# Segment mean over sorted ids: other places in the stream for looks, bridges and gathers, other places in the queue for the probes, and seven fills on ScalarE

## The chip, the cores and the metric

One core of one Trainium2 chip runs the kernel. The time is device microseconds of one execution. The engines are named as in the profile: DVE (VectorE), ACT (ScalarE), POOL (GpSimd, which also issues the indirect transfers), PE (TensorE, hardly used here) and SP (SyncE, which issues the plain transfers).

## The reference

Ten million values belong to 10,000 segments. The ids are sorted, so a segment is a contiguous stretch of about 1,000 values, and the result is the mean of each stretch:

```
sums = np.zeros(num_segments); counts = np.zeros(num_segments)
np.add.at(sums, segment_ids, data)
np.add.at(counts, segment_ids, 1)
return sums / np.maximum(counts, 1)
```

## The kernel before

Each of the 128 partitions holds 78,125 neighbouring values, cut into 90 **ranges** of 875. Two ranges make a data **tile** (128 x 1750 values, 875 KB); 45 tiles are loaded by SP in the order of `ORDER`: first the even tiles 0, 2, 4, 6, 8, then an odd and an even one in turn. The tile pool has 16 buffers. A range is taken to hold at most one segment boundary. ACT sums each tile (`total`, L557); DVE sums each range up to its boundary (`split`, L566, one instruction per range, 90 in all). Nothing of the ids is loaded whole. Where the boundary lies is found in three ways:

- **Probes** (`load_probes` L211, `load_mids` L216): SP fetches the id of every 175th position, 8 bytes at a time.
- **First look and second look**, for the ranges of even tiles: from the probes DVE works out which 175 ids hold the boundary and writes their places to `IDX` (L403). POOL gathers these ids with one indirect transfer per range (`gather`, L343), ACT adds them up (`add_ids`, L429) and DVE turns the sum into the exact place (`second_look`, L439).
- **Bridge**, for the ranges of odd tiles: with the exact places of the even neighbours on both sides, DVE guesses the boundary by a line between them (`bridge`, L481 to L524; LK at L481 is its first step, IDX at L519 its last but one). POOL gathers 232 ids around the guess, ACT adds them, `bridged` (L532) makes the place exact. Before a bridge POOL works out six small helpers (`prepare`, L455 to L468).

The even tiles are taken in nine **groups**, g0 to g8, of 1, 2, 3, 3, 3, 3, 3, 3 and 2 tiles, with two ranges per tile; a bridge goes with each group from g1 on. The gathered ids lie in a ring of 18 places (`RING`).

Every engine runs its instructions in the order in which the program writes them. The program is written **slot** by slot: slot s holds first the `add_ids` planned for it, then (for even s) the `total` of the next tile, then split s, and then the DVE and POOL steps put behind it (`after[s]`). The table `PLAN` has one row per group: slot and pace of the first look, slot of `prepare`, first slot of the adds of the 175 ids, slot of the second look, slot and pace of the bridge, first slot of the adds of the 232 ids, and slot of `bridged`. A pace of 99 puts all steps into one slot, a pace of 1, 2 or 3 so many steps into each. The first `HEAD` groups are looked at ahead of split 0. The table `POS` does the same for the steps that make counts, sums and outputs. SP's order comes from a list of pieces: each probe transfer has a slot, each data tile too, and a lead (`X_PIECE`, `X_DATA`) says how far ahead they are issued. At most eight of SP's transfers are under way, since the program has eight semaphores for them, and the next waits for the one eight before it; the gathers have eight of their own.

Of the kernel before, what the change touches and what calls it, by code (L numbers as in the profile page):

```python
# [9 lines left out]
FP32 = mybir.dt.float32  # L10
# [12 lines left out]
NR = 90  # L23
# [6 lines left out]
NX = NR + E  # L30
# [9 lines left out]
SEQ = [2 * t + k for t in ORDER for k in (0, 1)]  # L40
AT = {r: s for s, r in enumerate(SEQ)}
GROUPS = [(0, 1), (1, 3), (3, 6), (6, 9), (9, 12), (12, 15), (15, 18), (18, 21), (21, 23)]
X_PIECE = 22
X_DATA = 27
PLAN = [
# [9 lines left out]
]  # L55
POS = {
    "extend": (27, 1),
    "ext_rows": (42, 99),
    "keys": (38, 1),
    "keysx": (40, 2),  # L60
    "taxes": (50, -2),
    "counts0": (52, 2),
    "sums0": (59, 1),
    "head": (69, 2),
    "keys1": (51, 3),
    "counts1": (61, 1),
    "sums1": (62, 1),
    "place": (72, 1),
    "keys2": (59, -2),
    "check": (61, 1),  # L70
    "pick": (77, 2),
    "last": (78, 1),
    "counts2": (76, 2),
    "hits": (81, 1),
    "sums2": (79, 2),
    "spread2": (81, 1),
    "counts3": (81, 3),
    "verdict": (86, -2),
    "verdict1": (87, 1),
    "values": (89, 1),  # L80
    "weights": (82, -2),
    "base": (81, 99),
    "base2": (85, 1),
    "late": (86, 1),
    "place0": (70, 1),
    "recheck": (80, 1),
    "spans": (76, 1),
    "total": (88, 1),
}
# [85 lines left out]
def kernel(  # L175
# [6 lines left out]
    nc = tc.nc  # L182
# [9 lines left out]
    cpool = ctx.enter_context(tc.tile_pool(name="cpool", bufs=1))  # L192
# [35 lines left out]
    q5 = cpool.tile([P, 5, NX + PAD], FP32, name="q5")  # L228
# [5 lines left out]
    def view(ap, dims):  # L234
        return bass.AP(ap.tensor, ap.offset, [list(ap.ap[0])] + dims)

    nc.scalar.activation(  # L237
        out=gt32[:, :, 0 : 2 * WO : 2], in_=view(q5[:, 0, 0:1], [[0, RING], [0, WO]]), func=ACT.Copy
# [30 lines left out]
        out=plast, in0=pc, scalar1=float(P - 1), scalar2=1.0e6, op0=ALU.is_equal, op1=ALU.mult  # L269
# [5 lines left out]
        out=sp_i, in0=sp_i, scalar1=3, scalar2=None, op0=ALU.arith_shift_right  # L275
# [79 lines left out]
    def limits(a, b):  # L355

        def s1():
            need('VI', range(a, min(b + 1, NR)))
            nc.vector.tensor_sub(out=BT[:, a:b], in0=VI[:, a + 1 : b + 1], in1=VI[:, a:b])  # L359

        def s2():
            nc.vector.tensor_scalar(
                out=NB[:, a:b], in0=BT[:, a:b], scalar1=1.0, scalar2=None, op0=ALU.not_equal
            )
            mark('NB', range(a, b))

        return [s1, s2]

    def first_look(i, j):

        last = j == NE
        v = nc.vector
        e = lambda t: own(t, i, j)
        l1, l2 = limits(max(4 * i - 1, 0), min(4 * j - 1, NR))

        def s0():
            if last:
                m = NR * K + 1 - NPR
                v.tensor_copy(
                    out=pr_flat.bitcast(I32)[:, 2 * NPR : 2 * (NPR + m)].rearrange("p (a b) -> p a b", b=2),  # L380
                    in_=view(snt32[:, 0:1], [[0, m], [1, 2]]),
                )
            l1()

        def s1():
            v.tensor_reduce(
                out=e(SG), in_=view(pr32[:, 4 * i, 0:1], [[8 * K, j - i], [2 * K, 2], [2, K]]), axis=AX.X, op=ALU.add
            )

        def s2():  # L390
            v.scalar_tensor_tensor(
                out=e(ST), in0=view(pr32[:, 4 * i + 1, 0:1], [[8 * K, j - i], [2 * K, 2]]), scalar=float(K),
                in1=e(SG), op0=ALU.mult, op1=ALU.subtract,
            )

        def s3():
            need('NB', rows_of(i, j, 0))
            v.scalar_tensor_tensor(
                out=e(ST), in0=e(NB), scalar=FAR, in1=e(ST), op0=ALU.mult, op1=ALU.add
            )  # L400

        def s4():
            v.scalar_tensor_tensor(  # L403
                out=e(IDX), in0=e(ST), scalar=float(S), in1=e(wb), op0=ALU.mult, op1=ALU.add
            )
            if last:
                c = slice(NR - 1, NR)
                v.scalar_tensor_tensor(
                    out=IDX[:, c], in0=ST[:, c], scalar=float(TAIL), in1=wb[:, c], op0=ALU.mult, op1=ALU.add
                )  # L410
            for r in rows_of(i, j, 0):
                gather(r, W)

        def s5():
# [789 lines left out]
    head = len(after[-1])  # L1204
# [21 lines left out]
    t = table(M1, NT1 // 7, tax)  # L1226
# [107 lines left out]
```

## Time and profile before

| | before |
|---|---|
| median of 3 runs | 203.32 us (203.28 to 204.47) |
| the profiled execution, time / span | 204.23 us / 202.5 us |
| DVE busy | 144.7 us (71%), 479 instructions |
| ACT busy | 129.1 us (64%) |
| POOL busy | 120.1 us (59%), 90 gathers of them |
| DMA | 56.69 MB, of these 16.26 MB by the gathers |

The profiled execution took 1.8 us more than its span, and is 0.9 us above the median. The busy shares are averages; which wait ends last has to be read stretch by stretch.

### The profile page before, as it was taken

To read this page: it belongs to the slowest core of one execution; us is meant where nothing else is said; L and a number is where in the kernel's file an instruction comes from. 1 tells how busy PE (TensorE), PEld (TensorE's weight loads), DVE (VectorE), ACT (ScalarE), POOL (GpSimd) and SP (SyncE) were. 2 spreads that over 40 slices of the span, in tenths; PEclk is the share of its full clock that TensorE was granted. 3 is DMA by queue.
4 is the path that set the end of the run, shared out by engine and by line. 5 is a ranking of instruction groups with operands and counts; after the bars stand their busy time and mean duration, and the time that the engine had idled before them with its cause. 6 is when DMAs were issued, how large, how long until landed. Compare 5 with 4: busy or idle time off the path is not lost.

```text
span 202.5 us, 1502 instructions
## 1 busy us (share of the span) xinstructions
PE 1.6 (1%) x6; PEld 1.4 (1%) x6; DVE 144.7 (71%) x479; ACT 129.1 (64%) x283; POOL 120.1 (59%) x183
## 2 busy tenths in 40 slices
PE   0000000000000000100000000000000000000100
PEld 0000000000000000100000000000000000000000
DVE  6540391580599950995957999296999899999972
ACT  8100586551879953966599992666788995891250
POOL 5557777567577065586557177727477606964910
DMA  4979999999999999999999999999999902300000
GB/s 6 182 40 380 344 316 379 341 353 370 373 343 388 366 243 351 389 365 337 382 362 346 373 412 412 409 402 414 405 410 401 394 35 69 97 0 0 0 0 11
DMA packets 47684, 56.69 MB, mean 280 GB/s; under 512 B 37664, under 2 KB 38104, under 8 KB 47671
## 3 DMA queue, kind: packets, MB, share of 16 engines
q1 hardware_dynamic: 41739, 40.32, 60.1%
q0 software_dynamic: 5760, 16.26, 22.5%
q14 instruction: 13, 0.11, 0.1%
q10 hardware_dynamic: 172, 0.00, 0.0%
HBM read 58.97 MB, written 0.04 MB: 291 GB/s over the span
## 4 chain that ended last, share of the span: by engine, by line
DMA 30%; DVE 26%; issue 22%; ACT 9%; POOL 7%; SPq 2%; DVEq 0%; ACTq 0%; POOLq 0%
DMA GT<-in_segment_ids_dram,IDX 17%; DVE junk_v L566 15%; DMA data_t<-in_data_dram 11%; ACT junk_a L557 5%; POOL GT L343 5%; ACT junk_a L429 4%; DMA pr<-in_segment_ids_dram 2%; POOL xa L1056 2%; DVE PS L855 1%; SPq L211 1%; ACT add L1144 1%; POOL pb L1088 1%; DVE ct L863 1%; DVE most L1133 1%; DVE q L439 1%
## 5 line engine op out<-in xcount | busy, mean ns | idle before, releaser
L343 POOL DMA_INDIRECT GT<-in_segment_ids_dram,IDX x90 | 90.9, 1010 | 63.0 <-issue 24.3
L566 DVE SCALAR_TENSOR_TENSOR junk_v<-iota,q,data_t 128x875 bf16<-128x875 f32 x90 | 100.3, 1115 | 0.7
L557 ACT ACTIVATE junk_a<-data_t 128x1750 bf16<-128x1750 f32 (+1 forms) x45 | 74.2, 1650 | 1.4
L429 ACT ACTIVATE junk_a<-GT 128x175 bf16<-128x175 int32 (+1 forms) x90 | 34.5, 383 | 56.4 <-DMA GT<-in_segment_ids_dram,IDX 51.8
L439 DVE SCALAR_TENSOR_TENSOR q<-YY,GS 128x6 f32<-128x6 f32 (+2 forms) x9 | 1.5, 163 | 23.2 <-ACT junk_a L429 22.9
L429 ACT ACTIVATION_READ_ACCUMULATOR junk_a<-GT 128x1 f32 x90 | 16.8, 187 | 0.0
L532 DVE TENSOR_TENSOR q<-ZV,GS 128x6 f32<-128x6 f32 (+1 forms) x8 | 1.3, 162 | 14.8 <-ACT junk_a L429 14.8
L557 ACT ACTIVATION_READ_ACCUMULATOR junk_a<-data_t 128x1 f32 x45 | 8.4, 187 | 0.0
L566 DVE DVE_READ_ACCUMULATOR junk_v<-iota,q,data_t 128x1 f32 x90 | 7.3, 81 | 0.0
L831 ACT ACTIVATE junk_a<-bad 128x272 bf16<-128x272 f32 x1 | 0.4, 430 | 7.6 <-POOL OUT L1062 7.6
L481 DVE TENSOR_TENSOR LK<-q,LN 128x6 f32<-128x6 f32 (+1 forms) x8 | 1.3, 160 | 5.0 <-issue 5.0
L359 DVE TENSOR_TENSOR q<-pr 128x12 f32<-128x12 int32 (+3 forms) x9 | 1.6, 175 | 3.6 <-DMA pr<-in_segment_ids_dram 3.5
L237 ACT ACTIVATE GT<-q 128x4176 int32<-128x4176 f32 x1 | 3.9, 3908 | 0.0
L1056 POOL TENSOR_TENSOR xa<-xa 128x36 f32<-128x36 f32 (+3 forms) x5 | 3.5, 700 | 0.3
L286 DVE CAST jj<-jj_i 128x128 f32<-128x128 int32 x1 | 2.9, 2854 | 0.7 <-POOL jj_i L285 0.7
L855 DVE TENSOR_TENSOR_SCAN PS<-ps,PS 128x20 f32<-128x20 f32 (+2 forms) x4 | 2.8, 708 | 0.1
L1088 POOL TENSOR_TENSOR pb<-pb,RB 128x620 f32<-128x620 f32 x1 | 1.3, 1298 | 2.7 <-DVE RB L873 2.7
L1036 POOL TENSOR_TENSOR xa<-pa,RG 128x720 f32<-128x720 f32 x1 | 1.6, 1636 | 1.5 <-DVE RG L1032 1.5
L462 POOL TENSOR_TENSOR FB<-FB,wb 128x6 f32<-128x6 f32 (+1 forms) x8 | 1.7, 213 | 0.7
L468 POOL TENSOR_TENSOR WV<-wb,WV 128x6 f32<-128x6 f32 (+1 forms) x8 | 1.6, 202 | 0.7
L459 POOL TENSOR_SCALAR FB<-NBP 128x6 f32<-128x6 f32 (+1 forms) x8 | 1.6, 204 | 0.6
L1133 DVE TENSOR_REDUCE most<-add 128x31 f32<-128x930 f32 x1 | 1.1, 1121 | 1.2 <-ACT add L1144 1.2
(158 smaller groups left out, 81.6 us busy)
## 6 DMA issues: line engine op xcount, KB each, us to landing
data_t<-in_data_dram SPq DMA_DIRECT2D x44, 875.0 KB
GT<-in_segment_ids_dram,IDX POOLq DMA_INDIRECT x90
data_t<-in_data_dram SPq DMA_DIRECT2D x1, 562.5 KB
pr<-in_segment_ids_dram SPq DMA_DIRECT2D x22, 11.0 KB
pr<-in_segment_ids_dram SPq DMA_DIRECT2D x3, 6.0 KB
out_dram<-OUT SPq DMA_DIRECT2D x1, 36.6 KB
pr<-in_segment_ids_dram SPq DMA_DIRECT2D x1, 4.0 KB
snt<-in_segment_ids_dram ACTq DMA_DIRECT2D x1, 1.0 KB
```

The costliest lines, as they stand in the source:

```text
L211: nc.sync.dma_start(out=pr_flat[:, a:b], in_=ids_p[:, a * S : (b - 1) * S + 1 : S])
L237: nc.scalar.activation(out=gt32[:, :, 0 : 2 * WO : 2], in_=view(q5[:, 0, 0:1], [[0, RING], [0, WO]]), func=ACT.Copy)
L286: nc.vector.tensor_copy(out=jj, in_=jj_i)
L343: nc.gpsimd.indirect_dma_start(out=GT[:, slots[r], 0:w], out_offset=None, in_=ids2d[:], in_offset=bass.IndirectOffsetOnAxis(ap=IDX[:, r : ...
L429: nc.scalar.activation(out=junk_a[:, 0:w], in_=gt32[:, slots[r], 0 : 2 * w : 2], func=ACT.Copy, accum_out=GS[:, r : r + 1],)
L439: nc.vector.scalar_tensor_tensor(out=e(KK), in0=e(YY), scalar=float(S // K), in1=e(GS), op0=ALU.mult, op1=ALU.subtract)
L557: nc.scalar.activation(out=junk_a[:, 0:n], in_=tiles[t][:, 0:n], func=ACT.Copy, accum_out=T[:, 2 * t : 2 * t + 1])
L566: nc.vector.scalar_tensor_tensor(out=junk_v[:, 0:n], in0=iota[:, 0:n], scalar=KK[:, r : r + 1], in1=d, op0=ALU.is_ge if r % 2 else ALU.is_ ...
L855: nc.vector.tensor_tensor_scan(out=PS[:, a + 1 : b + 1], data0=ps, data1=ps, initial=PS[:, a : a + 1], op0=ALU.max, op1=ALU.max,)
L1056: nc.gpsimd.tensor_tensor(out=m[:, :, 0 : w - h], in0=m[:, :, 0 : w - h], in1=m[:, :, h:w], op=ALU.add)
L1088: e.tensor_tensor(out=pb, in0=pb, in1=view(RB[:, RM : RM + 1], [[0, NC], [1, NW]]), op=ALU.mult)
L1133: nc.vector.tensor_reduce(out=most, in_=add, axis=AX.X, op=ALU.add)
```

## The change

`PLAN` and `POS` get other numbers. `HEAD` is 2, so that the look of g2 moves behind the second look of g0. The look of g0 asks for three probes of its first tile alone (`limits(0, 2)`) and that of g1 for the rest; before, the look of g0 needed a fourth id, which a `load_mids` brings. The probe transfers, of which the first three stood ahead of all data and six more ahead of the second tile, now stand one to three at a time between data tiles. Seven buffers that POOL and its `memset` filled with zeros are filled by ACT, from a zero column of `q5`. `EARLY` is used nowhere.

```diff
-X_PIECE = 22
-X_DATA = 27
+X_PIECE = 24
+Y_PIECE = 0.75
+X_DATA = 26
 PLAN = [
...
-    (2, 1, 3, 3, 4, 4, 2, 10, 17),
-    (1, 99, 14, 5, 9, 20, 2, 25, 29),
+    (-1, 99, 3, 3, 4, 4, 2, 10, 17),
+    (1, 2, 13, 5, 10, 18, 99, 28, 28),
...
-HEAD = 3
-EARLY = 5
+HEAD = 2
+EARLY = 3
...
-        l1, l2 = limits(max(4 * i - 1, 0), min(4 * j - 1, NR))
+        l1, l2 = limits(*((0, 2) if j == 1 else (2 if i == 1 else 4 * i - 1, min(4 * j - 1, NR))))
...
-    nc.gpsimd.memset(tab, 0.0)
-    nc.gpsimd.memset(tax, 0.0)
-    nc.gpsimd.memset(shf[:, :, ND : ND + 1], 0.0)
-    nc.gpsimd.memset(add, 0.0)
-    nc.gpsimd.memset(xa, 0.0)
+    bad = cpool.tile([P, 2 * NX + 8 + 2 * NOD], FP32, name="bad")
+    for t in (tab, tax, shf[:, :, ND : ND + 1], add, xa, nbw, bad):
+        shape = [[0, n] for _, n in list(t.ap)[1:]]
+        nc.scalar.activation(out=t, in_=view(q5[:, 0, 0:1], shape), func=ACT.Copy)
...
-    nc.gpsimd.memset(nbw, 0.0)
...
-    pieces = [(load_probes, (i,), -99 if i < 3 else max(AT[4 * i] - X_PIECE , 1)) for i in range(NE)]
-    pieces += [(load_mids, (0, 4), 0.5)]
-    pieces += [(load_mids, (i, min(i + 6, NOD)), AT[4 * i] - X_PIECE - 1) for i in range(4, NOD, 6)]
+    at = lambda i: max(AT[4 * i] - X_PIECE, 0.5 + (i - 1) * Y_PIECE) if i else -99
+    pieces = [(load_probes, (i,), at(i)) for i in range(NE)]
+    pieces += [(load_mids, (i, min(i + 6, NOD)), at(i + 1) - 0.1) for i in range(4, NOD, 6)]
+    pieces += [(load_mids, (0, 4), 0.4)]
```

**POOL, from its last fills to the gathers of the second bridge.** GT with 175 are gathers of looks, GT with 232 those of bridges; LN, FB, SM and WV are the helpers of `prepare`, with two tiles (2x2) for the bridge of g1 and three (3x2) for that of g2. First before, then now:

```order
L632 MEMSET bad 128x272
L343 DMA GT<-in_segment_ids_dram,IDX 128x175 x12
L455 TENSOR_SCALAR LN<-NBP 128x2x2
L459 TENSOR_SCALAR FB<-NBP 128x2x2
L462 TENSOR_TENSOR FB<-FB,wb 128x2x2
L463 TENSOR_TENSOR SM<-q_74 128x2
L464 TENSOR_SCALAR WV<-pr 128x2x2
L468 TENSOR_TENSOR WV<-wb,WV 128x2x2
L343 DMA GT<-in_segment_ids_dram,IDX 128x175 x6
L455 TENSOR_SCALAR LN<-NBP 128x3x2
```

```order
L629 MEMSET KEY 128x112
L344 DMA GT<-in_segment_ids_dram,IDX 128x175 x6
L456 TENSOR_SCALAR LN<-NBP 128x2x2
...
L344 DMA GT<-in_segment_ids_dram,IDX 128x175 x6
L456 TENSOR_SCALAR LN<-NBP 128x3x2
...
L344 DMA GT<-in_segment_ids_dram,IDX 128x175 x6
L344 DMA GT<-in_segment_ids_dram,IDX 128x232 x10
```

Each `prepare` moved ahead of six gathers; that of g2 stood behind the gathers of g3 and now stands ahead of them.

**ACT, in the slots 21 to 29 of before.** The adds of g4 (175) and of the bridge of g3 (232) between the totals of the tiles (`data_t`). First before, then now:

```order
L429 ACTIVATE junk_a,GS<-GT 128x175 x3
L557 ACTIVATE junk_a,T<-data_t 128x1750
L429 ACTIVATE junk_a,GS<-GT 128x175 x2
L557 ACTIVATE junk_a,T<-data_t 128x1750
L429 ACTIVATE junk_a,GS<-GT 128x232 x2
L429 ACTIVATE junk_a,GS<-GT 128x175
L429 ACTIVATE junk_a,GS<-GT 128x232
```

```order
L430 ACTIVATE junk_a,GS<-GT 128x175 x3
L558 ACTIVATE junk_a,T<-data_t 128x1750
L430 ACTIVATE junk_a,GS<-GT 128x175 x3
L558 ACTIVATE junk_a,T<-data_t 128x1750 x2
L430 ACTIVATE junk_a,GS<-GT 128x232 x6
```

The last add of g4 stood behind two adds of the bridge and now stands ahead of all six.

**SP, the first transfers.** pr with 11 are probes, with 4 and 6 the single ids of `load_mids`, data_t the tiles. First before, then now:

```order
L211 DMA pr<-in_segment_ids_dram 128x11x1 x3
L216 DMA pr<-in_segment_ids_dram 128x6x1
L223 DMA data_t<-in_data_dram 128x1750
L216 DMA pr<-in_segment_ids_dram 128x4x1
L211 DMA pr<-in_segment_ids_dram 128x11x1 x6
L223 DMA data_t<-in_data_dram 128x1750 x2
```

```order
L212 DMA pr<-in_segment_ids_dram 128x11x1
L224 DMA data_t<-in_data_dram 128x1750
L217 DMA pr<-in_segment_ids_dram 128x4x1
L212 DMA pr<-in_segment_ids_dram 128x11x1 x3
L224 DMA data_t<-in_data_dram 128x1750
L212 DMA pr<-in_segment_ids_dram 128x11x1
L217 DMA pr<-in_segment_ids_dram 128x6x1
L212 DMA pr<-in_segment_ids_dram 128x11x1
L224 DMA data_t<-in_data_dram 128x1750
```

One probe instead of three stands ahead of the first tile, and the second tile has four probes ahead of it instead of nine.

The other moves, in words (slots before, then now). The places of a first look are all written in slot 47, then 48 for g7, in 25, then 23 for g5, in 39, then 35 for g6. The bridge of g3 ran over the slots 20 to 23 and stands whole in 18; that of g4 over 29 to 31 and stands whole in 29; that of g5 begins in 42, then 40; that of g6 in 53, then 52; that of g8 in 72, then 69. The second looks stand in 9, 25, 34, 48 (g3 to g6), now in 10, 24, 32, 47, and those of g7 and g8 stay in 56 and 68; `bridged` stands in 29, 40, 53 (g3 to g5), now in 28, 41, 52.

## Rows read from the trace of the kernel before

**Rows 1.** Page, parts 1, 3 and 5: engines, a DMA queue (packets, MB), gathers.

```profile
PE 1.6 (1%) x6; PEld 1.4 (1%) x6; DVE 144.7 (71%) x479; ACT 129.1 (64%) x283; POOL 120.1 (59%) x183
...
q0 software_dynamic: 5760, 16.26, 22.5%
...
L343 POOL DMA_INDIRECT GT<-in_segment_ids_dram,IDX x90 | 90.9, 1010 | 63.0 <-issue 24.3
```

**Rows 2.** Timeline of DVE, waits: start, us, instruction, shapes [idle before <-releaser].

```profile
10.24 0.17 DVE L359 TENSOR_TENSOR q<-pr 128x3 f32<-128x3 int32 x1 [2.50 <-DMA pr<-in_segment_ids_dram]
...
21.15 0.16 DVE L439 SCALAR_TENSOR_TENSOR q<-YY,GS 128x2 f32<-128x2 f32 x1 [7.23 <-ACT junk_a L429]
...
37.69 0.17 DVE L481 TENSOR_TENSOR LK<-q,LN 128x6 f32<-128x6 f32 x1 [4.98 <-issue]
...
52.44 0.16 DVE L532 TENSOR_TENSOR q<-ZV,GS 128x4 f32<-128x4 f32 x1 [7.39 <-ACT junk_a L429]
...
80.73 0.17 DVE L439 SCALAR_TENSOR_TENSOR q<-YY,GS 128x6 f32<-128x6 f32 x1 [7.21 <-ACT junk_a L429]
...
96.34 0.17 DVE L439 SCALAR_TENSOR_TENSOR q<-YY,GS 128x6 f32<-128x6 f32 x1 [2.47 <-ACT junk_a L429]
107.26 0.17 DVE L532 TENSOR_TENSOR q<-ZV,GS 128x6 f32<-128x6 f32 x1 [3.43 <-ACT junk_a L429]
...
131.48 0.17 DVE L532 TENSOR_TENSOR q<-ZV,GS 128x6 f32<-128x6 f32 x1 [3.72 <-ACT junk_a L429]
...
139.58 0.17 DVE L439 SCALAR_TENSOR_TENSOR q<-YY,GS 128x6 f32<-128x6 f32 x1 [1.91 <-ACT junk_a L429]
```

**Rows 3.** Timeline of POOL: some of its gathers, and one helper (LN).

```profile
12.01 1.27 POOL L343 DMA_INDIRECT GT<-in_segment_ids_dram,IDX  x1 [4.36 <-DVE YY L415]
...
26.63 1.00 POOL L343 DMA_INDIRECT GT<-in_segment_ids_dram,IDX  x1 [0.30 <-issue]
27.70 0.20 POOL L455 TENSOR_SCALAR LN<-NBP 128x4 f32<-128x4 f32 x1
...
29.78 1.09 POOL L343 DMA_INDIRECT GT<-in_segment_ids_dram,IDX  x1 [0.59 <-DVE LL L488]
...
41.67 1.08 POOL L343 DMA_INDIRECT GT<-in_segment_ids_dram,IDX  x1 [2.83 <-DVE CC L514]
...
71.63 1.08 POOL L343 DMA_INDIRECT GT<-in_segment_ids_dram,IDX  x1 [5.43 <-ACT junk_a L429]
```

**Rows 4.** Timeline of ACT: the first fill, and adds that waited for a gather.

```profile
2.04 3.91 ACT L237 ACTIVATE GT<-q 128x4176 int32<-128x4176 f32 x1
...
15.89 0.36 ACT L429 ACTIVATE junk_a<-GT 128x175 bf16<-128x175 int32 x1 [9.94 <-DMA GT<-in_segment_ids_dram,IDX]
...
32.07 0.36 ACT L429 ACTIVATE junk_a<-GT 128x175 bf16<-128x175 int32 x1 [0.18 <-DMA GT<-in_segment_ids_dram,IDX]
...
78.84 0.41 ACT L429 ACTIVATE junk_a<-GT 128x232 bf16<-128x232 int32 x1 [5.12 <-DMA GT<-in_segment_ids_dram,IDX]
```

**Rows 5.** Timeline of DVE, start: two casts.

```profile
2.97 0.21 DVE L254 CAST rp<-rp_i 128x110 f32<-128x110 int32 x1
...
4.88 2.85 DVE L286 CAST jj<-jj_i 128x128 f32<-128x128 int32 x1 [0.73 <-POOL jj_i L285]
```

**Rows 6.** Timeline of DVE: splits 29, 41, 54, 57 and the last instruction.

```profile
85.05 1.13 DVE L566 SCALAR_TENSOR_TENSOR junk_v<-iota,q,data_t 128x875 bf16<-128x875 f32 x1
...
108.25 1.12 DVE L566 SCALAR_TENSOR_TENSOR junk_v<-iota,q,data_t 128x875 bf16<-128x875 f32 x1
...
132.61 1.03 DVE L566 SCALAR_TENSOR_TENSOR junk_v<-iota,q,data_t 128x875 bf16<-128x875 f32 x1
...
140.49 1.12 DVE L566 SCALAR_TENSOR_TENSOR junk_v<-iota,q,data_t 128x875 bf16<-128x875 f32 x1
...
198.21 0.27 DVE L1157 SCALAR_TENSOR_TENSOR OUT<-gb,q,most 128x31 f32<-128x31 f32 x1
```

**Rows 7.** One stretch: us, length; busy PE, PEld, DVE, ACT, POOL; PEclk, DMA share, GB/s.

```profile
0.00:120.00 120.00, 0.98 (x4) 0.93 (x4) 75.19 (x259) 76.69 (x169) 74.06 (x120) 1.00 1.01 321
```

More of the change, by code (lines that the diff above doesn't have):

```diff
@@ L42 @@
 GROUPS = [(0, 1), (1, 3), (3, 6), (6, 9), (9, 12), (12, 15), (15, 18), (18, 21), (21, 23)]
-X_PIECE = 22
-X_DATA = 27
+X_PIECE = 24
+Y_PIECE = 0.75
+X_DATA = 26
 PLAN = [
[9 rows of a table removed]
[9 rows of a table added]
 ]
 POS = {
-    "extend": (27, 1),
-    "ext_rows": (42, 99),
-    "keys": (38, 1),
+    "extend": (30, 1),
+    "ext_rows": (45, 99),
+    "keys": (35, 99),
     "keysx": (40, 2),
     "taxes": (50, -2),
-    "counts0": (52, 2),
-    "sums0": (59, 1),
-    "head": (69, 2),
+    "counts0": (50, 2),
+    "sums0": (61, 1),
+    "head": (72, 99),
     "keys1": (51, 3),
[L66 to L70, printed above, removed]
+    "counts1": (54, 1),
+    "sums1": (63, 1),
+    "place": (71, 1),
+    "keys2": (60, 3),
+    "check": (61, -2),
     "pick": (77, 2),
-    "last": (78, 1),
-    "counts2": (76, 2),
-    "hits": (81, 1),
+    "last": (77, 2),
+    "counts2": (76, 1),
+    "hits": (82, -2),
     "sums2": (79, 2),
@@ L79 @@
     "verdict1": (87, 1),
-    "values": (89, 1),
-    "weights": (82, -2),
+    "values": (89, 2),
+    "weights": (82, 1),
     "base": (81, 99),
     "base2": (85, 1),
-    "late": (86, 1),
-    "place0": (70, 1),
+    "late": (87, -2),
+    "place0": (72, 1),
     "recheck": (80, 1),
-    "spans": (76, 1),
-    "total": (88, 1),
-}
-HEAD = 3
-EARLY = 5
+    "spans": (74, 3),
+    "total": (88, 99),
+}
+HEAD = 2
+EARLY = 3
 RING = 18
@@ L621 @@
     nc.vector.memset(RF, 0.0)
-    nc.gpsimd.memset(tab, 0.0)
-    nc.gpsimd.memset(tax, 0.0)
-    nc.gpsimd.memset(shf[:, :, ND : ND + 1], 0.0)
-    nc.gpsimd.memset(add, 0.0)
-    nc.gpsimd.memset(xa, 0.0)
+    bad = cpool.tile([P, 2 * NX + 8 + 2 * NOD], FP32, name="bad")
+    for t in (tab, tax, shf[:, :, ND : ND + 1], add, xa, nbw, bad):
+        shape = [[0, n] for _, n in list(t.ap)[1:]]
+        nc.scalar.activation(out=t, in_=view(q5[:, 0, 0:1], shape), func=ACT.Copy)
     nc.vector.memset(PS[:, 0:1], 0.0)
     nc.vector.memset(PX[:, 0:1], 0.0)
-    nc.gpsimd.memset(nbw, 0.0)
     nc.gpsimd.memset(KEY, -1000.0)
-    bad = cpool.tile([P, 2 * NX + 8 + 2 * NOD], FP32, name="bad")
-    nc.gpsimd.memset(bad, 0.0)
     j1 = cpool.tile([P, NX], FP32, name="j1")
```

14 rows, old and new, of the table PLAN are left out of this document.

## The prediction, made before the changed kernel ran

> **What bounds the kernel now.** I read the busy shares first: no engine is busy for more than 71% of the span, and 90 gathers with 16.26 MB run beside the data [rows 1]. An average of 71% hides two halves, so I went on to the waits of DVE, which ends the kernel [rows 2]. They stand between 10 and 140 us, and nearly all have one releaser: the ACT add of a gathered set of ids. The large ones are 7.23 us at 21.15 (second look of g0), 4.98 at 37.69 (LK, the first step of the bridge of g2), 7.39 at 52.44 (`bridged` of g1), 7.21 at 80.73 (second look of g4), then 2.47, 3.43, 3.72 and 1.91. Split 57 starts at 140.49 and the last DVE instruction at 198.21 [rows 6]; the waits of that tail that I read are short, so I take its 57.7 us as DVE's own work. POOL tells why the adds are late [rows 3]: gathers follow each other at (26.63 - 12.01) / 11 = 1.33 us, so POOL is the metronome of the first 60 us, and its first gather goes out only at 12.01. A gather lands some time later, seen where an ACT add waits for it [rows 4]: 12.01 to 15.89 = 3.9 us for the first, 26.63 to 32.07 = 5.4, 71.63 to 78.84 = 7.2. So the first half is a chain: look on DVE, gather on POOL, landing, add on ACT, second look on DVE. What starts it earlier, or takes a queue out of it, moves all behind it, up to the point where another resource binds.
>
> **The change, part by part.** All times are in the profiled execution's own span.
>
> *Start.* Before, the first wait of DVE ends at 10.24, for probes, and the gather follows 1.77 later [rows 2, 3]. Two things now come earlier. The cast of `jj` took 2.85 us beside POOL's fills, a like cast 0.21 [rows 5]; with the fills gone from POOL it should take about 0.2, and DVE stands at the look from about 4.88 + 0.3 = 5.2. And the look of g0 needs only the one probe transfer ahead of the first data tile. When that lands no row shows: at the earliest DVE is ready at 5.2, at the latest it is 10.24 again. I take 5.5, near the first, since one transfer stands where three stood with a tile before the fourth id: gather 0 at 5.5 + 1.8 = 7.3. ACT's seven fills hold 2839 elements per partition; at 3.91 us for 4176 [rows 4] that is 2.7 us, up to 4 with seven starts. They end near 10, ahead of the first landing at 7.3 + 3.9 = 11.2, which is their cover; without it they would cost at most those 4 us once.
>
> *g0 to g2.* g1's look needs the later probes; I put it at 9 and its four gathers at 10.4 to 15.7. Gather 1 (8.6) lands at 12.5 to 15.8, so the second look of g0 stands at 13.2 to 16.5, and the look of g2, now behind it, 1.8 later. POOL meanwhile does `prepare` of g1, which takes 27.70 to about 29.2, 1.5 us [rows 3]. g2's gathers so start between 17.4 and 18.2; I take 17.8. Before, they were the seventh to twelfth in the row: 12.01 + 6 x 1.33 = 20.0. The gain is only 2.2, since the wait of 7.23 gets a successor of its own.
>
> The first landing of 3.9 us was measured while few gathers were under way, the 7.2 in the saturated stretch [rows 4]. The Trainium skill, page "DMA: Bandwidth & Descriptors", section "Queues, rings and completion order", says that each DMA engine goes round-robin between the queue rows that have work, packet by packet. By it an earlier gather shares every engine with the tiles at once, and this speaks against the whole gain of an earlier start; with 7.2 instead of 3.9 the second look of g0 stands at 16.5 and g2's gathers start at 18.2, 0.4 later than the sum has them. No run here shows yet which it is.
>
> *The bridge of g1.* Before, `prepare` of g2 stood behind g3's six gathers, and LK waited 4.98 for it. Now it stands ahead of them: g2's gathers end at 17.8 + 8.0 = 25.8, `prepare` at 27.1 to 27.3, g3's gathers at 35.1. LK's wait goes, and the bridge of g1 has its places written by then, so its first gather is at 35.1 (41.67 before [rows 3]). Its `bridged` ended its wait 52.44 - 41.67 = 10.77 after that; the same behind 35.1 gives 45.8. Gain 6.6; with the places 1.3 late, 5.3.
>
> *g3, g4, bridge of g3.* Sixteen gathers (four and six of two bridges, six of g4) take 35.1 + 21.3 = 56.4; the second look of g3, now in slot 10, waits about 1.3 for an add that stands ahead of it, and the gathers of g4 slip by some 1.7; `prepare` adds 1.5, the bridge of g3 in one piece about 1.2. Its first gather is at 60.8, before at 71.63 [rows 3]. On ACT the last add of g4 no longer stands behind adds of the bridge: that order was the wait of 7.21 at 80.73 [rows 2]. So DVE runs 45.8 + (85.05 - 52.44 - 7.21) + 1.3 + 0.5 = 73.0 on its own work to split 29 [rows 2, 6], while the last gather of the bridge, at 67.4, needs 7.2 to land and 0.6 for the add, 75.2: a new wait of some 2.2, split 29 at 75.4. **Gain 9.6.**
>
> *g5.* Its gathers run from 67.4 + 1.33 + 1.5 = 70.3 to 77.0; with 7.2 + 0.6 the second look of g5 stands at 84.8, a wait of about 3. Before, from that step at 96.34 six splits took 108.25 - 96.34 - 3.43 = 8.48, 1.41 each; now eight splits follow, 11.3, and some four small steps that moved ahead, at 0.99 / 5 = 0.2 each (the five between 107.26 and 108.25 [rows 2, 6]). Split 41 at 84.8 + 11.3 + 0.8 = 96.9. **Gain 11.35.**
>
> *Splits 41 to 57.* Before 132.61 - 108.25 - 3.72 = 20.64 of work to split 54 [rows 2, 6]; seven steps have moved in (1.4): 118.9. Its wait of 3.72 should vanish, the gathers of that bridge having the two slots by which it begins earlier. To split 57 there are 140.49 - 132.61 - 1.91 = 5.97, four more steps (0.8) and a wait of 1.5 to 2, since the second look of g7 stays in its slot: 127.5. **Gain 13.0.**
>
> *The tail.* 57.7 us less the 1.2 of six steps now ahead of it. Gain 14.2 at most. Against that I set 1.2: at 120 us the stream has moved 120 x 321 = 38.5 MB [rows 7], and splits 54 to 56, now near 120, need 28 tiles, which come just in time. **Gain 13.0**: 204.23 - 13.0 = 191.2 in the profile's own time, which stands 0.9 above the median of the runs; so 190.3, and I say **190.5 us**.
>
> The spread probes, the casts and the moved table steps of the tail add no instruction. The probe transfers pass data tiles in SP's queue; before, no split waited for data, so a tile delayed by 11 KB transfers costs nothing as long as that slack lasts, which is what the 1.2 and the first rival are for.
>
> **Rivals.**
>
> (a) *The data stream becomes the bound.* At about 118 us some 37.9 MB have moved. Of these about 69 gathers take 69 x 16.26 / 90 = 12.5 MB [rows 1], which leaves 25.4 MB, or 28 tiles of 0.9 MB, several of them in flight, not landed. Split 53 needs 27 whole tiles. For it: a faster DVE does not raise the 321 GB/s [rows 7]. Against: no split before waited for a tile. If DVE is held by about 5 us there, the end is near 195.5. Chance 0.16.
>
> (b) *The bunched adds bring waits back.* `bridged` of g3 and g5 and the second look of g5 stand in slots 28, 52 and 32 behind adds of a whole group; if landings take 2 to 3 us longer than 7.2 at three of them, 8 us go: 198.5. For it: every wait in the list has this releaser. Against: gathers themselves start 8 to 11 us earlier there. Chance 0.10.
>
> (c) *The gain is handed back entirely*, by (a) and (b) in turn or because g0's probe lands at 10 us as before: 201.5 to 205. Chance 0.09.
>
> (d) *Slower.* All looks stand in DVE's order ahead of splits that need nothing of them. The probes that a look reads now wait in SP's queue behind data tiles, and some looks come earlier (g5 in slot 21, before 24; `Y_PIECE` and `X_PIECE` place the transfer). A look that meets an absent probe stops DVE, its splits and its gathers too. The only such wait before was 2.50 at 10.24 [rows 2]. It decides once it eats the whole 13 and 2 more: about 3 us at each of five looks, which gives 206 to 210. For it: eight transfers at a time, each tile 0.9 MB or 2.8 us at 321 GB/s, so a probe behind eight places lands 22 us after its turn. Against: `X_PIECE` of 24 slots, at 1.2 us or more, leaves 29. Chance 0.09.
>
> **How the numbers follow.** The forecast has 0.56. The lower end is the forecast less what I allowed for: without the 1.2 for data, the 2.2 at split 29 and 1 at the start, 186. The upper end must take in (a) and (b), 200, and leaves out (c), (d) and a little. Range **186 to 200**. About 1% (2 us) is what a measurement of this kernel can tell from no change. Faster by over 1%, below 201.3: the forecast, (a) and (b), 0.82. Within 1%: most of (c), 0.08. Slower: (d) and the rest, 0.10.
>
> **What the new profile would show.** The cast of `jj` at 0.2 us, the first gather at 7.3, the first wait that an ACT add ends no later than 16.5; no wait at LK of g2; `bridged` of g1 at 45.8; no wait of 7 us at the second look of g4; splits 29, 41, 54 and 57 at 75.4, 96.9, 118.9 and 127.5; the last DVE instruction at 185. Wrong: a wait of DVE or ACT whose releaser is `data_t` shows (a), one at L360 for `pr` shows (d), waits above 4 us at slots 28, 32 or 52 show (b). If the first gather stays near 12 us the start has failed and the rest shrinks by up to 4.5 us.

## The result and the profile after

The changed kernel takes **187.08 us** (median of 4 runs, 185.92 to 188.99) against 203.42 beside it; the ratio is 0.916 with a 95% interval of 0.909 to 0.923. Ratios here and below are taken over the fast runs alone (here without 188.99 and with a fifth run of 186.27), so they are not the quotients of the medians shown. A second comparison gave 187.17 us and 0.920 (0.913 to 0.927). Forecast were 190.5 us and a range of 186 to 200. The profiled execution took 188.09 us with a span of 186.3.

The page of the changed kernel first, parts 1 and 5 (busy us, mean ns | idle time ahead and what ended most of it):

```profile
PE 1.6 (1%) x6; PEld 1.4 (1%) x6; DVE 143.3 (77%) x479; ACT 131.9 (71%) x290; POOL 117.3 (63%) x176
...
L567 DVE SCALAR_TENSOR_TENSOR junk_v<-iota,q,data_t 128x875 bf16<-128x875 f32 x90 | 100.6, 1118 | 5.7 <-DMA data_t<-in_data_dram 5.1
...
L440 DVE SCALAR_TENSOR_TENSOR q<-YY,GS 128x6 f32<-128x6 f32 (+2 forms) x9 | 1.5, 171 | 12.3 <-ACT junk_a L430 12.3
L533 DVE TENSOR_TENSOR q<-ZV,GS 128x6 f32<-128x6 f32 (+1 forms) x8 | 1.9, 232 | 9.0 <-ACT junk_a L430 9.0
L360 DVE TENSOR_TENSOR q<-pr 128x12 f32<-128x12 int32 (+3 forms) x9 | 1.6, 175 | 6.1 <-DMA pr<-in_segment_ids_dram 6.0
```

Two lines of the page before, for the splits and for the first step of the looks:

```profile
L566 DVE SCALAR_TENSOR_TENSOR junk_v<-iota,q,data_t 128x875 bf16<-128x875 f32 x90 | 100.3, 1115 | 0.7
...
L359 DVE TENSOR_TENSOR q<-pr 128x12 f32<-128x12 int32 (+3 forms) x9 | 1.6, 175 | 3.6 <-DMA pr<-in_segment_ids_dram 3.5
```

DVE is busy for nearly as long as before (143.3 us, 144.7 in [rows 1]) and for a larger share, so what was saved is waiting. What waiting is left for adds is 12.3 + 9.0 us, and a new kind has come: 5.1 us for data tiles, where before no split waited for one. The looks wait 6.1 us, mostly for probes, where it was 3.6.

The timeline of DVE in the changed kernel (columns as in [rows 2]): the cast of `jj`, the larger waits, and two steps that no longer wait, LK of g2 at 30.05 and the second look of g4 at 66.37:

```profile
4.87 0.23 DVE L287 CAST jj<-jj_i 128x128 f32<-128x128 int32 x1 [0.72 <-POOL jj_i L286]
...
8.78 0.17 DVE L360 TENSOR_TENSOR q<-pr 128x9 f32<-128x9 int32 x1 [2.59 <-DMA pr<-in_segment_ids_dram]
15.03 0.16 DVE L440 SCALAR_TENSOR_TENSOR q<-YY,GS 128x2 f32<-128x2 f32 x1 [5.32 <-ACT junk_a L430]
16.42 0.18 DVE L360 TENSOR_TENSOR q<-pr 128x12 f32<-128x12 int32 x1 [1.23 <-DMA pr<-in_segment_ids_dram]
...
29.78 0.17 DVE L440 SCALAR_TENSOR_TENSOR q<-YY,GS 128x6 f32<-128x6 f32 x1 [2.26 <-ACT junk_a L430]
30.05 0.17 DVE L482 TENSOR_TENSOR LK<-q,LN 128x6 f32<-128x6 f32 x1
...
45.54 0.20 DVE L533 TENSOR_TENSOR q<-ZV,GS 128x4 f32<-128x4 f32 x1 [6.87 <-ACT junk_a L430]
...
66.37 0.23 DVE L440 SCALAR_TENSOR_TENSOR q<-YY,GS 128x6 f32<-128x6 f32 x1
...
71.39 1.13 DVE L567 SCALAR_TENSOR_TENSOR junk_v<-iota,q,data_t 128x875 bf16<-128x875 f32 x1 [1.33 <-DMA data_t<-in_data_dram]
74.67 0.23 DVE L533 TENSOR_TENSOR q<-ZV,GS 128x6 f32<-128x6 f32 x1 [2.15 <-ACT junk_a L430]
82.74 0.17 DVE L440 SCALAR_TENSOR_TENSOR q<-YY,GS 128x6 f32<-128x6 f32 x1 [1.17 <-ACT junk_a L430]
95.08 1.13 DVE L567 SCALAR_TENSOR_TENSOR junk_v<-iota,q,data_t 128x875 bf16<-128x875 f32 x1 [2.63 <-DMA data_t<-in_data_dram]
...
124.85 0.17 DVE L440 SCALAR_TENSOR_TENSOR q<-YY,GS 128x6 f32<-128x6 f32 x1 [0.46 <-ACT junk_a L430]
```

Against [rows 2]: the wait at LK and that of 7.21 us at the second look of g4 are gone. `bridged` of g1 still waits, 6.87 us, but ends at 45.54 instead of 52.44. The waits of 3.43 and 3.72 at `bridged` of g4 and g5 are gone too.

POOL in the changed kernel: the first gather, the first and last of g2, the first of the bridges of g1 and g3:

```profile
7.07 1.26 POOL L344 DMA_INDIRECT GT<-in_segment_ids_dram,IDX  x1 [2.10 <-DVE YY L416]
...
17.57 1.09 POOL L344 DMA_INDIRECT GT<-in_segment_ids_dram,IDX  x1 [1.18 <-DVE IDX L404]
...
24.17 0.99 POOL L344 DMA_INDIRECT GT<-in_segment_ids_dram,IDX  x1 [0.30 <-issue]
...
35.14 0.99 POOL L344 DMA_INDIRECT GT<-in_segment_ids_dram,IDX  x1 [0.30 <-DMA GT<-in_segment_ids_dram,IDX]
...
59.80 1.08 POOL L344 DMA_INDIRECT GT<-in_segment_ids_dram,IDX  x1 [1.84 <-ACT junk_a L558]
```

They answer to [rows 3]: 12.01 became 7.07, 41.67 became 35.14, 71.63 became 59.80. ACT in the changed kernel, the last fill and the add of the first gather (as [rows 4]):

```profile
8.52 0.41 ACT L626 ACTIVATE bad<-q 128x272 f32<-128x272 f32 x1
13.44 0.36 ACT L430 ACTIVATE junk_a<-GT 128x175 bf16<-128x175 int32 x1 [4.51 <-DMA GT<-in_segment_ids_dram,IDX]
```

The fills end at 8.9, with 4.51 us to spare. The first gather took 13.44 - 7.07 = 6.4 us to land, 3.9 before. The Trainium skill, page "DMA: Bandwidth & Descriptors", section "Queues, rings and completion order", has each DMA engine go round-robin between the queues that have work; the trace agrees in so far as a gather among tiles and probes took nearer 7.2 than 3.9; between issue and add the DMA engines moved 204 GB/s now and 96 before.

The splits 29, 41, 54 and 57 and the last instruction of DVE in the changed kernel (as [rows 6]):

```profile
74.83 1.12 DVE L567 SCALAR_TENSOR_TENSOR junk_v<-iota,q,data_t 128x875 bf16<-128x875 f32 x1
...
97.30 1.13 DVE L567 SCALAR_TENSOR_TENSOR junk_v<-iota,q,data_t 128x875 bf16<-128x875 f32 x1
...
119.20 1.13 DVE L567 SCALAR_TENSOR_TENSOR junk_v<-iota,q,data_t 128x875 bf16<-128x875 f32 x1 [0.20 <-DMA data_t<-in_data_dram]
...
126.44 1.13 DVE L567 SCALAR_TENSOR_TENSOR junk_v<-iota,q,data_t 128x875 bf16<-128x875 f32 x1
...
182.01 0.27 DVE L1154 SCALAR_TENSOR_TENSOR OUT<-gb,q,most 128x31 f32<-128x31 f32 x1
```

The lead is 10.2 us at split 29, 11.0 at 41, 13.4 at 54, 14.1 at 57 and 16.2 at the end.

### The profile page after: what moved, and what is told of

It is laid out like the page before. It is cut to its first block, busy times and chain, and to the rows that moved or that the text cites. A ratio compares the mean times of both kernels' runs of the same rounds, so it can differ in the third digit from the quotient of the medians.

```text
span 186.3 us, 1505 instructions
## 1 busy us (share of the span) xinstructions
PE 1.6 (1%) x6; PEld 1.4 (1%) x6; DVE 143.3 (77%) x479; ACT 131.9 (71%) x290; POOL 117.3 (63%) x176
## 4 chain that ended last, share of the span: by engine, by line
SPq 31%; DMA 27%; DVE 23%; issue 12%; ACT 3%; POOL 2%; DVEq 0%; POOLq 0%; ACTq 0%
SPq L224 20%; DMA data_t<-in_data_dram 17%; DVE junk_v L567 13%; SPq L212 9%; DMA pr<-in_segment_ids_dram 6%; DMA GT<-in_segment_ids_dram,IDX 4%; POOL GT L344 1%; ACT add L1141 1%; SPq L217 1%; DVE PS L852 1%; ACT junk_a L430 1%; ACT junk_a L558 1%; DVE most L1130 1%; DVE pa L1017 0%; DVE shf L983 0%
## 5 line engine op out<-in xcount | busy, mean ns | idle before, releaser
L440 DVE SCALAR_TENSOR_TENSOR q<-YY,GS 128x6 f32<-128x6 f32 (+2 forms) x9 | 1.5, 171 | 12.3 <-ACT junk_a L430 12.3
L533 DVE TENSOR_TENSOR q<-ZV,GS 128x6 f32<-128x6 f32 (+1 forms) x8 | 1.9, 232 | 9.0 <-ACT junk_a L430 9.0
L360 DVE TENSOR_TENSOR q<-pr 128x12 f32<-128x12 int32 (+3 forms) x9 | 1.6, 175 | 6.1 <-DMA pr<-in_segment_ids_dram 6.0
L1088 DVE TENSOR_TENSOR_SCAN gg<-nbw,PX,pb 128x620 f32<-128x620 f32 x1 | 2.1, 2086 | 0.0
L456 POOL TENSOR_SCALAR LN<-NBP 128x6 f32<-128x6 f32 (+1 forms) x8 | 1.6, 199 | 0.6
```

The source lines that it names most:

```text
L533: nc.vector.tensor_sub(out=odd(KK, i, j), in0=odd(ZV, i, j), in1=odd(GS, i, j))
L1088: nc.vector.tensor_tensor_scan(out=back(gg), data0=back(nbw), data1=back(pb), initial=PX[:, 0:1], op0=ALU.mult, op1=ALU.add,)
```

## The experiments

Ratios are to the kernel before on the same chip, with 95% intervals. The changed kernel stands at 0.916 (0.909 to 0.923) and, run again, 0.920 (0.913 to 0.927).

> The changed kernel once more, on the chip and beside the runs that the next kernels share: 0.91 to 0.92 of before, as in the first comparison (0.916).

As expected. In its profile DVE waited 1.3 us for data tiles instead of 5.1, and its span was 1.2 us shorter. `bridged` of g1 ended its wait 1.1 us later than in the first profile:

```profile
46.65 0.16 DVE L533 TENSOR_TENSOR q<-ZV,GS 128x4 f32<-128x4 f32 x1 [9.19 <-ACT junk_a L430]
```

Three runs below with the same start (two tiles fewer, the rows of g5 to g8 back, the old `POS`) have it at 46.43 to 46.65. So a mark of a single trace is good to about 1 us, and 45.54 is an early one. The chain that ended last (part 4 of the page) is another too, first in the first profile, then in the repeat:

```profile
SPq L224 20%; DMA data_t<-in_data_dram 17%; DVE junk_v L567 13%; SPq L212 9%; DMA pr<-in_segment_ids_dram 6%; DMA GT<-in_segment_ids_dram,IDX 4%; POOL GT L344 1%; ACT add L1141 1%; SPq L217 1%; DVE PS L852 1%; ACT junk_a L430 1%; ACT junk_a L558 1%; DVE most L1130 1%; DVE pa L1017 0%; DVE shf L983 0%
...
DMA GT<-in_segment_ids_dram,IDX 13%; DVE junk_v L567 13%; POOL GT L344 9%; DMA data_t<-in_data_dram 5%; ACT junk_a L430 4%; ACT junk_a L558 4%; DMA pr<-in_segment_ids_dram 3%; ACT add L1141 1%; DVE PS L852 1%; DVE most L1130 1%; SPq L212 1%; DVE pa L1017 0%; DVE shf L983 0%; SPq L224 0%; DVE xa L993 0%
```

One runs mostly through SP's issues and the tiles, the other mostly through the gathers, and the two executions took 188.09 and 186.91 us. This fits two chains that end nearly together.

**The order alone.** The rows of `PLAN` for g3 to g8 and `POS` as changed; the fills, the looks of g0 to g2 and all of SP's queue as before:

```diff
 PLAN = [ ...rows g0 to g2 as before...
-    (1, 99, 14, 5, 9, 20, 2, 25, 29),
+    (1, 2, 13, 5, 10, 18, 99, 28, 28),
...
```

> The kernel before with the changed rows of PLAN for g3 to g8 and the changed POS alone; probes, the looks of g0 to g2 and the fills stay as they were. Theory (most of the gain is the order of gathers, helpers and adds; the earlier start carries on as far as the gathers are the bound): gathers of g2 from 20.0 us, helpers of g2 ahead of the gathers of g3, first gather of the bridge of g1 near 38.7, its wait at bridged ends near 49.5 (before 52.4, changed 45.5); the end about 4 us behind the changed kernel at most, 188 to 191.5. Rival (the start is the main thing): the end stays within 3 us of before, 200 to 204.

190.14 us, ratio 0.928 (0.919 to 0.937). DVE, `bridged` of g1 and split 29:

```profile
50.92 0.16 DVE L532 TENSOR_TENSOR q<-ZV,GS 128x4 f32<-128x4 f32 x1 [9.62 <-ACT junk_a L429]
...
78.69 1.12 DVE L566 SCALAR_TENSOR_TENSOR junk_v<-iota,q,data_t 128x875 bf16<-128x875 f32 x1
```

The time is where the theory had it, so the order is most of the gain. Its first marks came late: the first gather of the bridge of g1 at 39.56 (38.7 expected), the end of the wait at `bridged` of g1 at 50.92 (49.5). Behind the first profile of the changed kernel it is by 5.4 us there, 3.9 at split 29 and 1.9 at split 57 (128.29): more than half of what the start adds is gone by split 57.

**The start alone.** The old rows for g3 to g8 and the old `POS` in the changed kernel:

> The changed kernel with the old rows of PLAN for g3 to g8 and the old POS; probes, the looks of g0 to g2 and the fills as changed. Theory: the wait at LK of g2 and the 7 us wait at the second look of g4 come back; bridged of g1 near 48.7 instead of 52.4, and these 3 to 4 us carry to the end: 199 to 201. Rival 1 (the start is the main thing): 190 to 195. Rival 2 (a lead at the start is swallowed by the next wait): 202.5 to 204.

200.33 us, ratio 0.979 (0.972 to 0.986), as the theory has it. Its DVE timeline shows the two waits that the changed order takes away, at LK of g2 and at the second look of g4, and between them that at `bridged` of g1, which stays and ends 3.4 us earlier in the changed kernel:

```profile
33.41 0.17 DVE L482 TENSOR_TENSOR LK<-q,LN 128x6 f32<-128x6 f32 x1 [3.72 <-POOL LN L456]
48.93 0.17 DVE L533 TENSOR_TENSOR q<-ZV,GS 128x4 f32<-128x4 f32 x1 [8.15 <-ACT junk_a L430]
77.04 0.17 DVE L440 SCALAR_TENSOR_TENSOR q<-YY,GS 128x6 f32<-128x6 f32 x1 [7.02 <-ACT junk_a L430]
```

The lead of 3.5 us that the start gives at `bridged` of g1 (48.93, before 52.44) is carried to the end whole: the last DVE instruction stands at 194.43, before at 198.21.

**Only the fills back.**

```diff
-        nc.scalar.activation(out=t, in_=view(q5[:, 0, 0:1], shape), func=ACT.Copy)
+        nc.gpsimd.memset(t, 0.0)
```

> The changed kernel with its seven fills on POOL again. Theory: the cast of jj takes 2.8 us again, the first gather goes out near 9.7 instead of 7.07, but the look of g2 waits for its probes until 16.4 in any case, so bridged of g1 moves by 1 us at most and the time by 0 to 1: 187 to 188.3. Rival (the chain starts with this cast): the 2.6 us are carried to the end, 189.5 to 190.5.

190.32 us, ratio 0.931 (0.924 to 0.938). My theory fell: all its runs lie above 189.5, and it stands 1.2 to 1.6% behind the changed kernel (0.920 and 0.916), as far as the run with the whole old start (0.928); its interval is just clear of that of the first comparison and overlaps that of the second. The rival's time came, but not by its 2.6 us. Its trace, first DVE, then POOL (the first gather, the first and the last of g2), then ACT (the add of that last one):

```profile
4.88 1.90 DVE L287 CAST jj<-jj_i 128x128 f32<-128x128 int32 x1 [0.73 <-POOL jj_i L286]
...
32.66 0.17 DVE L440 SCALAR_TENSOR_TENSOR q<-YY,GS 128x6 f32<-128x6 f32 x1 [5.49 <-ACT junk_a L430]
...
48.71 0.22 DVE L533 TENSOR_TENSOR q<-ZV,GS 128x4 f32<-128x4 f32 x1 [8.28 <-issue]
```

```profile
8.72 1.26 POOL L344 DMA_INDIRECT GT<-in_segment_ids_dram,IDX  x1 [0.97 <-DVE YY L416]
...
18.60 1.09 POOL L344 DMA_INDIRECT GT<-in_segment_ids_dram,IDX  x1 [0.53 <-issue]
...
25.22 1.00 POOL L344 DMA_INDIRECT GT<-in_segment_ids_dram,IDX  x1 [0.30 <-issue]
```

```profile
32.17 0.36 ACT L430 ACTIVATE junk_a<-GT 128x175 bf16<-128x175 int32 x1 [2.60 <-DMA GT<-in_segment_ids_dram,IDX]
```

The cast takes 1.90 us where I had 2.8, the first gather is 1.65 us later where I had 2.6, and the first of g2 1.0. But the last of g2, issued at 25.22, lands 6.95 us later, while in the changed kernel the one issued at 24.17 was added at 29.30, 5.1 us later. So 1.0 us became 2.9 at the second look of g2 and 3.2 at `bridged` of g1, or 2.1 against the repeat. I had taken the landing of a gather for fixed, and it is not. Between issue and add the DMA engines moved 339 GB/s here and 237 in the changed kernel; that the fuller stream is the cause is not shown.

**Two data tiles fewer in the changed kernel.**

```diff
-            load_data(ORDER[nt])
+            if nt in (12, 18):
+                tiles[ORDER[nt]] = tiles[ORDER[nt - 1]]
+            else:
+                load_data(ORDER[nt])
```

> The changed kernel with two data tiles of the order (the 13th and the 19th) not loaded, the tile ahead of each read twice in their place; every instruction on DVE, ACT and POOL stays, and 1.8 MB of transfers, some 5.3 us of the stream, are left out. Theory (from about 70 to 123 us the stream of data tiles holds DVE and ACT): the waits of DVE for data_t, 5.1 us in sum, go, and the time falls by 2 to 5 us to 182 to 185. Rival (the gathers and their adds still set the pace): the chain of adds keeps its times and the time stays within 1 us, 186 to 188.

186.80 us, ratio 0.914 (0.907 to 0.921): not told apart from the changed kernel. The page's line for the splits:

```profile
L567 DVE SCALAR_TENSOR_TENSOR junk_v<-iota,q,data_t 128x875 bf16<-128x875 f32 x90 | 100.6, 1118 | 0.7
```

The waits for data are gone (idle time ahead of the 90 splits 0.7 us), and the waits at the second looks and `bridged` remain: 7.95 at 46.65, 2.01 at 74.06, 1.80 at 122.57. So the stream of tiles is not what sets the time by itself, though it does stop splits: take its 5.1 us of waits away, and the last DVE instruction comes only 2.3 us earlier than in the first profile (179.71) and 1.1 earlier than in the repeat (180.81), since some of the waits for gathers grow (1.80 at the second look of g7, 0.46 in the changed kernel). The theory's 2 to 5 us of time were wrong, and with them my first rival, the stream as the bound by itself.

**The largest wait of before alone.**

```diff
-    (9, 3, 22, 21, 25, 29, 3, 36, 40),
+    (9, 3, 22, 21, 24, 29, 3, 36, 40),
```

> The kernel before with one number changed: the second look of g4 and its last add go ahead of the adds of the bridge of g3 (slot 24 for 25), nothing else. Theory (the wait of 7.2 us at 80.7 stands for the late gathers of that bridge, whose last goes out at 78.2 and lands 7 us later): the wait moves to bridged of g3, split 29 starts at 84 to 85.3 instead of 85.05 and the time falls by 0 to 1 us: 202.5 to 204. Rival (the order on ACT is the cause of the wait): 5 to 7 us less, 196 to 198.5.

203.89 us, ratio 0.999 (0.996 to 1.002): nothing. DVE in this run:

```profile
82.56 0.17 DVE L585 TENSOR_TENSOR q<-T,q 128x10 f32<-128x10 f32 x1 [6.61 <-ACT junk_a L557]
86.21 0.17 DVE L532 TENSOR_TENSOR q<-ZV,GS 128x6 f32<-128x6 f32 x1 [0.97 <-ACT junk_a L429]
```

The wait of 7.21 did not vanish, it went to the next step that needs ACT: L585 wants a total that stands on ACT behind the adds of the bridge, whose gathers are as late as before. Split 29 (84.10) and the time came as the theory had them; the place of the new wait did not.

**The same, and the bridge of g3 earlier.**

```diff
-    (1, 99, 14, 5, 9, 20, 2, 25, 29),
-    (9, 3, 22, 21, 25, 29, 3, 36, 40),
+    (1, 99, 13, 5, 9, 18, 99, 28, 28),
+    (9, 3, 22, 21, 24, 29, 3, 36, 40),
```

> The kernel before with the same change and with the changed numbers for the bridge of g3: whole in slot 18, its adds all in slot 28. Theory (the start of the gathers of this bridge is what counts): its first gather at 64 to 65 instead of 71.6, split 29 at 78 to 79.5 instead of 85.05, and these 6 us carry to the end less 1 to 2 us at the later waits: 197.5 to 199.5. Rival (the next waits, on g5 and the bridge of g4 with their old rows, take the lead back): 201 to 204.

199.36 us, ratio 0.978 (0.973 to 0.983). POOL, the first gather of the bridge of g3, and DVE, where it is waited for:

```profile
66.55 1.08 POOL L343 DMA_INDIRECT GT<-in_segment_ids_dram,IDX  x1 [1.84 <-DVE IDX L519]
```

```profile
81.00 0.17 DVE L532 TENSOR_TENSOR q<-ZV,GS 128x6 f32<-128x6 f32 x1 [2.46 <-ACT junk_a L429]
```

The gather goes out at 66.55 (71.63 before), 1.5 to 2.5 us later than I had it, and split 29 at 81.08, so 4 us are won there, and 5.5 at the last DVE instruction (192.75); the time fell by some 2.2%. The order of the adds in the run above won nothing; with earlier gathers the time falls: the start of the gathers is what counts. This run moves the adds of the bridge to slot 28 as well, so the two are not wholly apart. By themselves those adds had little to give: in the run above, the last gather of the bridge goes out at 77.44, and with 7.2 us to land and 0.6 for the add `bridged` could not have come before 85.2, where it came at 86.21. That is an estimate from these rows.

**The helpers of g2 first, alone.**

```diff
-    (1, 99, 14, 5, 9, 20, 2, 25, 29),
+    (1, 2, 14, 5, 9, 20, 2, 25, 29),
```

> The kernel before with one number changed: the look of g3 at pace 2 (99 before), so that the helpers of g2 stand ahead of the six gathers of g3. Theory (that wait of 4.98 us at LK becomes a lead only as far as the gathers allow): LK waits no more, the gathers of g3 start 1.5 us later, the first gather of the bridge of g1 goes out at 38.9 instead of 41.7, bridged of g1 ends its wait at 49.7 to 51 (52.4), and 1.5 to 2.7 us are carried to the end: 201.5 to 203. Rival (the wait at LK is worth its length): 5 us, 199 to 200.

201.30 us, ratio 0.988 (0.983 to 0.992), as the theory has it. LK of g2 waits no more, and `bridged` of g1 waits longer:

```profile
50.16 0.17 DVE L532 TENSOR_TENSOR q<-ZV,GS 128x4 f32<-128x4 f32 x1 [10.40 <-ACT junk_a L429]
```

It ended its wait at 52.44 before, so the wait of 4.98 us at LK, taken away whole, is worth 2.3 there and 2 to 2.5 in the time. A wait is worth what the next one leaves of it.

**The rows of g5 to g8 back in the changed kernel.** (The text on record speaks of the bridges of g4 to g7; the rows put back hold looks and bridges of g5 to g8, so that of g4 kept its new numbers.)

> The changed kernel with the old rows of PLAN for g5 to g8 (looks, bridges of g4 to g7, their adds); all else as changed. Theory: with the old slots the waits of before at bridged of g4 and g5 and the second look of g7 (3.43, 3.72, 1.91) come back, split 29 stays near 74.5 and the time rises by 4 to 8 us, to 191 to 195. Rival (the stream of tiles holds DVE in that stretch anyway and hides them): 187 to 189.

188.40 us, ratio 0.927 (0.923 to 0.931): the rival's time came, about 1% behind the changed kernel, and the theory's 4 to 8 us didn't. At split 40 DVE stands for a data tile:

```profile
93.16 1.13 DVE L567 SCALAR_TENSOR_TENSOR junk_v<-iota,q,data_t 128x875 bf16<-128x875 f32 x1 [3.15 <-DMA data_t<-in_data_dram]
```

While it stands, the old rows lose little: the first gather of the bridge of g5 goes out at 101.55, in the changed kernel at 100.95, and `bridged` of g5 hardly waits:

```profile
117.35 0.19 DVE L533 TENSOR_TENSOR q<-ZV,GS 128x6 f32<-128x6 f32 x1 [0.32 <-ACT junk_a L430]
```

Split 57 begins at 124.73, in the changed kernel at 126.44; behind it 56.1 us lie between splits 57 and 89 against 54.4 there. That is for the most part work that stands elsewhere: from split 57 to the last DVE instruction DVE runs 172 instructions against 166, and that instruction comes at 182.03 against 182.01.

**The old `POS` in the changed kernel.**

> The changed kernel with the old POS, that is with the steps of counts, sums and outputs in their old slots. Theory (the tail from split 57 to the last instruction, 55.6 us against 57.7 before, gained by steps moved ahead and two shorter waits): 1 to 2.5 us more, 188.2 to 189.7. Rival (the same steps only lie elsewhere in the same DVE order): within 0.7 us, 186.5 to 188.

188.21 us, ratio 0.925 (0.918 to 0.932). Its interval covers the second ratio of the changed kernel (0.920) and misses the first (0.916) by a little, so what `POS` is worth is not settled; from split 57 to 89 it needs 55.2 us.

**Two attempts at a faster version.** First the early probes closer together (`Y_PIECE` 0.5 for 0.75):

> The changed kernel with Y_PIECE 0.5 for 0.75: the second tile has one probe transfer more ahead of it, the third has three more. Theory (the start carries to the end as the run with the fills on POOL showed, where 1.0 us at the gathers of g2 became 3.2 us at bridged of g1): the waits for probes at 16.4 and 23.1 (1.2 us each) go, bridged of g1 comes 1 to 2 us earlier and the time falls by 1 to 2 us. Rival 1 (the tiles are the bound in the middle and take the lead back): no change within 0.7 us. Rival 2: tiles 2 and 3 land too late for splits 4 to 6, slower by 1 us or more.

188.11 us, ratio 0.922 (0.917 to 0.926): the same as the changed kernel beside it (0.920), so the theory fell. The look of g2 waits 0.74 instead of 1.23, that of g3 no more, but the second look of g2 ends its wait at 30.32, and a wait of 2.83 us at `bridged` of g2 is new. Then later probes:

```diff
-X_PIECE = 24
+X_PIECE = 20
...
-    (8, 2, 22, 21, 24, 29, 99, 37, 41),
+    (9, 3, 22, 21, 24, 29, 99, 37, 41),
```

> An attempt at a faster version: the changed kernel with X_PIECE 20 for 24, so that the probes from the ninth tile on stand behind two more data tiles, and the look of g4 one slot later to give its probes time. Theory (tiles and gathers set the pace in turn): the waits of DVE for data_t go, the chain of gathers stays, and the time falls by 0 to 1.5 us: 185.7 to 187.2. Rival: a look waits for its probes, 188 to 190.

Slower: 189.82 us, ratio 0.933 (0.929 to 0.936). Its profile is of an execution of 192.68 us, so only the kind of wait is read from it. DVE:

```profile
112.00 0.18 DVE L360 TENSOR_TENSOR q<-pr 128x12 f32<-128x12 int32 x1 [3.88 <-issue]
```

That is the look of g7. The profile names no releaser; L360 reads `pr`, so I take it to be held at its probes, as the same look is in the run with the old rows of g5 to g8 (1.51 us, released by the probes' transfer). How much of the lost time this wait makes is not shown. No version was found that beats the changed kernel.

## Why the prediction was right, step by step

| step | forecast | before | measured |
|---|---|---|---|
| first gather | 7.3 | 12.01 | 7.07 |
| gathers of g2 begin | 17.8 | 20.11 | 17.57 |
| first gather of the bridge of g1 | 35.1 | 41.67 | 35.14 |
| `bridged` of g1 | 45.8 | 52.44 | 45.54 |
| first gather of the bridge of g3 | 60.8 | 71.63 | 59.80 |
| split 29 | 75.4 | 85.05 | 74.83 |
| split 41 | 96.9 | 108.25 | 97.30 |
| split 54 | 118.9 | 132.61 | 119.20 |
| split 57 | 127.5 | 140.49 | 126.44 |
| last DVE instruction | 185 | 198.21 | 182.01 |
| profiled time | 191.2 | 204.23 | 188.09 |

**Start.** Right, and for more than the sum gave it: 2.2 us at the gathers of g2, where the start alone brings 3.8 at the last DVE instruction. On top of the order it brings about 2 there (184.14 to 182.01). The cast of `jj` took 0.23 us. With the fills back on POOL the kernel is as slow as with the whole old start; that ACT's fills are hidden is shown by the 4.51 us that ACT waits behind them.

**g1 to g3.** The chain held to within 1 us at each of its marks. Of the two large waits, the one at LK was worth 2 to 2.5 us rather than its length, and the one at the second look of g4 nothing by itself. For that one the prediction's reason was wrong: it named the order of the adds on ACT as the cause, and that order alone won nothing. The mark at split 29 came right because the sum took the later of two ends there, the last gather of the bridge and its landing. The new wait at split 29 was forecast at 2.2 and is 2.15.

**g5, splits 41 to 57.** The marks are right, their reasons only in part. The second look of g5 came at 82.74, 2 us before the forecast, and a wait of 2.63 us for a data tile at split 40 took that back: that split 41 fits to 0.4 us is luck (in the repeat it begins at 95.44, 1.5 early). I had put the whole trouble with tiles, 1.2 us, near splits 54 to 56; it lies mostly at splits 28 and 40, and at 54 it is 0.20. I had also credited the two slots by which the bridge of g5 begins earlier with the wait of 3.72; with the old rows of g5 to g8 it is 0.32, so those slots are not needed for it. With the start alone it is 3.87; which part of the changed order or of the stand at split 40 removes it the runs don't separate.

**The tail** is the term that was mis-sized: I kept it at 57.7 us in sum (1.2 off for moved steps, 1.2 on for tiles), and it took 182.01 - 126.44 = 55.6. With 1.1 us at split 57 this is the whole difference of 3.1 between 191.2 and 188.09. I had also taken the 57.7 for DVE's own work. DVE was busy for 54.76 us of it, and for 53.92 of the 55.57 after: so 0.8 of the 2.15 us won is work, with seven instructions fewer behind split 57, and 1.3 is idle time that I had not looked at. No tile stopped a split there.

**The rivals.** (a) is half true: its sign is there, the tiles do hold splits and ACT's totals, and the rate did not rise (320 GB/s over the first 120 us, 321 before); but the run with two fewer shows no gain in the time beyond the noise. (b) did not come in the changed kernel. (d) has its mechanism: looks wait for probes, 6.1 us in all by the page where it was 3.6. That 3.6 holds a second wait, of 1.00 us at 12.97, beside the 2.50 that the prediction called the only one. Now it is 2.59, 1.23, 1.24 and 0.97 us at the looks of g1 to g4, short of the 3 at each of five looks at which it decides. (c) did not happen, though each half of the change alone gives 2% or 7%, together 8%.

## What to carry to other kernels

A long wait in the list is not a gain of its length: the one of 7.2 us was worth nothing and the one of 5.0 half, because the next step waited for late transfers too; ask when the waited-for transfers start, and move that. Write the marks of the chain down one after the other, each from a row, and check them one by one: the sum here was right to 3 us because each mark was, one of them by luck. The parts that weren't right were a stretch taken whole as work though 3 us of it were idle, and an allowance whose place was guessed (tiles at splits 54 to 56).
When two chains end nearly together, taking away one's waits need not move the time, as the run with two tiles fewer shows. And a mark of one trace, here good to about 1 us, needs a second trace before a difference is read from it.

## What was not expected of the hardware

The last gather of g2, 128 x 175 ids, took 5.1 us from issue to its add in the changed kernel and 6.95 with the fills on POOL, where it was issued 1.05 us later. Seven fills of 2839 elements per partition, moved from POOL to ACT, took ACT from 5.83 to 8.93 us; back on POOL they held a cast of 128 x 128 beside them for 1.90 us, which took 0.23 without them, and the whole kernel lost 1.2 to 1.6%.
